# First weights of the heads' values loaded and split inside the last seven-product units

## The chip, the cores and the metric

The kernel runs on one core of one Trainium2 chip. The metric is the device time of one execution in microseconds (us); the median over several runs counts. Five engines work side by side, each on its own queue, in order: TensorE (PE: matmuls and transposes, with its weight loads on PEld), VectorE (DVE), ScalarE (ACT), GpSimd (POOL) and SyncE (SP), which here only issues loads.

## The reference

One layer of a streaming-encoder trunk, 1024 tokens of width 1024, all in float32. What matters here is the start of it:

```python
h = rms_norm(x, g_mix[l])
proj = h @ w_in[l]
c_h, c_b, c_c, sq, sk, sv, xq, gate_pre = jnp.split(proj, split_idx, axis=-1)
...
kv = mem_n @ w_mem_kv
```

`sv` are the values of the 16 heads of the stick-breaking attention, 1024 tokens by 1024 columns. `mem_n` are 256 normalised memory tokens, and `kv` their keys and values for a second attention. After the mixers come a merge, an output product and an MLP.

## The kernel before

**Three matmuls a product.** Each float32 operand is split in a high half (a cast to fp32r) and a low half (the operand less the high half); a product is then three matmuls: high by high, high by low, low by high. For a weight piece of 128 x 1024, `load` (L83) issues the DMA on SP into a buffer `raw` (four exist), and `split_w` makes the high half on ACT (L89) and the low half on DVE (L90). `unit(src, True)` is a load with its split into two pages. A page is a buffer of 128 x 1024, `pg` in the profile; 40 exist. A buffer that is taken again waits until its last reader is done.

**The units.** Most columns of `proj` come from a class `Unit`: a 2 x 2 block product by seven products instead of eight (`p1` to `p7`, L284 to L288), each of 12 matmuls 128x512. The blocks of h are called 11, 21, 12, 22 (second digit: which half of the tokens), and T1 to T4 are sums and differences of them. T1 and T2 are read only by the pair `p6`, `p5`. A unit's own halves of the weights are made by `w1` to `w4`; all of these, and the copies and additions behind each product, go through helpers that pin their order (`order`, L240 on DVE, L243 on ACT).

**The drive.** `Drive.run` walks through a list of (pair, unit). The last six entries of the first drive, of 13 units, are (1,11), (1,12), (2,11), (2,12), (3,11), (3,12): the pairs `p1 p2`, `p6 p5` and `p7 p3`, and `p4` behind pair 3. So the products at the end are p6, p5 of unit 11, p6, p5 of unit 12, then p7, p3, p4 of unit 11 and p7, p3, p4 of unit 12. After the first and second product of each entry, `hook(n, 0)` and `hook(n, 1)` are called. A hook calls `late(n - NP, i)`, if there is one, and then a step of `fin`, the work that a unit leaves to DVE and ACT (here two products of whole pages, two scalings, four shifted additions L596, two more products, and stores). The first drive has no `late`; the second, in the MLP, has one.

```python
                hook(n, 0)
                ...
                second()
                hook(n, 1)
                if k == 3:
                    un.p4()
                    ends.append(un.fin())
```

**Behind the drive.** The block 12 comes back from DRAM (`h12scr`, two loads) and is split by ACT and DVE. Then `v_steps` makes the values: for each of two column groups, four weight pieces `w_v[cg, kp]`, and for each of eight token tiles j a product of 24 matmuls (L210 to L212) in a bank `d`, copied out by ACT (`vv`, L778). Token tiles 0 to 3 need the blocks 11 and 21, tiles 4 to 7 the blocks 12 and 22. The memory tokens (`in_mem`, two loads on SP) are squared on ACT (L157), normalised by DVE, POOL and DVE (L146, L150, L159), and then transposed on TensorE (L176) in between the tiles' matmuls. Loads and splits of `w_kv` follow, and of the second group of `w_v`.

The splits of `w_v` behind the drive are not pinned (`pin[0] = False`); there a scheduler chooses each engine's order.

Of the kernel before, what the change touches and what calls it, by code (L numbers as in the profile page):

```python
# [42 lines left out]
def block_kernel(ctx, tc, x, mem, small, w_in, w_v, w_kv, w_co, w_so, w_xo, w_out, w_up, w_dn, out):  # L43
# [15 lines left out]
    def nm(s):  # L59
        uid[0] += 1  # L60
        return f"{s}_{uid[0]}"
# [7 lines left out]
    def pd():  # L69
        return ps_d.tile([P, 512], F32, tag="d", name=nm("d"))  # L70
# [10 lines left out]
    def load(src):  # L81
        raw = rawp.tile([P, 1024], F32, tag="raw", name=nm("raw"))
        nc.sync.dma_start(out=raw, in_=src)  # L83
        return raw
# [11 lines left out]
    def halves(raw, paged=False):  # L96

        if paged:
            hl = (page(), page())
        else:  # L100
            w = whlp.tile([P, 2, 1024], F32R, tag="whl", name=nm("whl"))
            hl = (w[:, 0, :], w[:, 1, :])
        split_w(raw, hl)
        return hl

    def unit(src, paged=False):

        return halves(load(src), paged)
# [20 lines left out]
    def cut(hl, a, b):  # L129
        return (hl[0][:, a:b], hl[1][:, a:b])  # L130
# [22 lines left out]
    def normed(src):  # L153

        ss = stat(1)
        xn = page(F32)
        nc.scalar.activation(xn, src, AF.Square, accum_out=ss)  # L157
        r = rstd(ss, 1, D)
        nc.vector.tensor_scalar_mul(xn, src, r)  # L159
        return xn  # L160
# [45 lines left out]
    def mm3_steps(ps, pairs, cuts=2):  # L206

        n = len(pairs)
        for i, ((ah, al), (bh, bl)) in enumerate(pairs):
            nc.tensor.matmul(ps, lhsT=ah, rhs=bh, start=i == 0, stop=False)  # L210
            nc.tensor.matmul(ps, lhsT=ah, rhs=bl, start=False, stop=False)  # L211
            nc.tensor.matmul(ps, lhsT=al, rhs=bh, start=False, stop=i == n - 1)  # L212
            if (i + 1) % (n // cuts) == 0:
                yield
# [283 lines left out]
    sec_h = Seconds(C_GMIX, h12_scr)  # L498

    def hx(k, th):  # L500

        return sec_h.h[("11", "12", "21", "22")[2 * (k // 4) + th]][k % 4]
# [114 lines left out]
    def a_(sec, rows, kk):  # L617
        return lambda: sec.second_a(rows, kk)

    def b_(sec, kk):  # L620
        return lambda: sec.second_b(kk)

    def weaving(sec, rows):

        hooks = {at: a_(sec, rows, kk) for kk, at in enumerate(((0, 1), (1, 0), (1, 1), (2, 0)))}
        hooks.update({(4 + kk // 2, kk % 2): b_(sec, kk) for kk in range(4)})
        return hooks

    xrows = load_rows(x, 0, 4)
    dr = Drive(units)  # L630
# [2 lines left out]
    xrows = load_rows(x, 512, 4)  # L633
    run(sec_h.first(rows0))
    rows1 = [normed(t) for t in xrows]
    dr.run(weaving(sec_h, rows1))
    pin[0] = False


# [117 lines left out]

    def v_steps():

        us = [unit(w_v[0, kp], True) for kp in range(4)]  # L760
        for cg in range(2):
            un = []
            for j in range(8):
                if cg == 0 and j >= 4:
                    un.append(unit(w_v[1, j - 4], True))
                ps = pd()
                yield from mm3_steps(
                    ps,
                    [
                        (  # L770
                            cut(hx(k, j // 4), (j % 4) * P, (j % 4) * P + P),
                            cut(us[k // 2], (k % 2) * 512, (k % 2) * 512 + 512),
                        )
                        for k in range(KT)
                    ],
                )
                vv = hpp.tile([P, 512], F32, tag="hp", name=nm("vv"))
                nc.scalar.copy(vv, ps)  # L778
                nc.gpsimd.dma_start(
                    out=v_scr[cg][:, :, j * P : (j + 1) * P], in_=vv.rearrange("p (a e) -> p a e", a=4)  # L780
                )
            us = un
# [163 lines left out]

    nxt = {}
    vgen = v_steps()
    fill(vgen, 2)
    mts = [normed(t) for t in load_rows(mem, 0, NM)]  # L950
# [190 lines left out]
    for ch in range(2):  # L1141
# [3 lines left out]
        for t in range(8):  # L1145
            th, i = t // 4, t % 4
# [183 lines left out]
```

## Time and profile before

| | us |
|---|---|
| median of 3 runs | 2228.43 |
| lowest and highest | 2228.33, 2230.82 |
| the profiled execution | 2230.86 |
| its span, first to last instruction | 2229.2 |

The profiled execution has its own time, 1.7 us longer than its span, and 2.4 us above the median of the three runs. In the rows of a timeline the first number is the start in us from the span's start, the second the duration (of all of a merged group, where a count such as x2 stands at the end), and in brackets the idle time of the engine ahead of it with what ended that. In a table by windows the numbers behind the stretch are its length, the busy time of PE, PEld, DVE, ACT and, where it did anything, POOL, each with a count of instructions, then the granted clock of TensorE as a share of full speed, the DMA engines' mean busy share, and GB/s.

### The profile page before, as it was taken

Reading aid. Unit: us, or ns where it says so; the run is one execution under the profiler, and the core shown is the slowest. Engines: PE = TensorE matmul, PEld = TensorE weight load, DVE = VectorE, ACT = ScalarE, POOL = GpSimd, SP = SyncE. Lnnn points to the kernel's source line nnn. Section 1 sums busy time; section 2 is a strip of 40 time slices with the busy share of each in tenths; the row PEclk is TensorE's granted clock in tenths of the full one; section 3 lists DMA queues with packets and bytes.
Section 4 is the critical chain, followed back from the end, with each engine's and each line's share of the span. In section 5 each row is a group of like instructions: output and inputs, shape, how many; then the busy total and the mean of one; then the engine's idle time right before and its main releaser. Section 6 shows DMA issues by size and latency. Waiting matters only on the chain.

```text
span 2229.2 us, 27032 instructions
## 1 busy us (share of the span) xinstructions
PE 2164.5 (97%) x10148; PEld 1789.0 (80%) x10148; DVE 1405.1 (63%) x1891; ACT 1002.9 (45%) x1789; POOL 383.8 (17%) x574
## 2 busy tenths in 40 slices
PE   7999989999999999999999999999989999999999
PEld 5788869888888788778888788888868888788887
DVE  6555552265778778778777534442576565777776
ACT  6333243354656555555655321121555555433332
POOL 1000011122333333333333000000112211200000
PEclk9999999999999999999999999999999999999999
DMA  4322243232312222321221445334234444744444
GB/s 170 132 66 76 84 173 126 82 122 90 99 67 65 90 74 60 94 75 57 91 80 68 150 151 161 104 95 161 104 133 165 147 148 171 265 162 142 142 151 142
DMA packets 75011, 263.94 MB, mean 118 GB/s; under 512 B 9856, under 2 KB 9856, under 8 KB 74880
## 3 DMA queue, kind: packets, MB, share of 16 engines
q1 hardware_dynamic: 53824, 190.37, 26.6%
q0 software_dynamic: 21056, 71.84, 8.5%
q8 instruction: 80, 1.31, 0.2%
q14 instruction: 51, 0.42, 0.1%
HBM read 181.95 MB, written 71.83 MB: 114 GB/s over the span
## 4 chain that ended last, share of the span: by engine, by line
PE 72%; DVE 11%; issue 7%; ACT 6%; POOL 4%; DMA 1%; POOLq 0%; ACTq 0%; DVEq 0%; SPq 0%
PE d L211 6%; PE d L212 6%; PE d L210 6%; PE d L287 6%; PE d L288 6%; PE d L284 6%; PE d L126 4%; PE d L127 4%; PE d L125 4%; PE z L288 4%; PE z L284 4%; PE z L287 4%; DVE pg L240 3%; POOL pg L847 2%; DVE pg L114 2%
## 5 line engine op out<-in xcount | busy, mean ns | idle before, releaser
L210 PE MATMUL d<-pg,whl 128*128 128x512 f32 x736 | 294.6, 400 | 0.1
L243 ACT ACTIVATE pg<-pg 128x512 f32<-128x512 f32 (+1 forms) x192 | 150.6, 790 | 306.2 <-DVE pg L240 293.5
L211 PE MATMUL d<-pg,whl 128*128 128x512 f32 x736 | 288.1, 391 | 0.0
L212 PE MATMUL d<-pg,whl 128*128 128x512 f32 x736 | 288.1, 391 | 0.0
L847 POOL TENSOR_SCALAR_AFFINE_SELECT pg<-pg 128x128 f32<-128x128 f32 x256 | 168.8, 666 | 282.1 <-ACT pg L844 270.8
L857 DVE TENSOR_TENSOR_SCAN pg<-pg,zero 128x128 f32<-128x128 f32 (+7 forms) x128 | 177.1, 1383 | 57.2 <-POOL pg L847 54.5
L240 DVE TENSOR_TENSOR pg<-pg,pg 128x1024 fp32r<-128x1024 f32 (+3 forms) x180 | 183.5, 1030 | 46.6 <-ACT pg L243 42.9
L113 ACT CAST pg<-t 128x256 fp32r<-128x256 f32 (+2 forms) x336 | 115.1, 368 | 203.3 <-DVE pg L114 144.7
L284 PE MATMUL d<-pg,whl 128*128 128x512 f32 x420 | 166.3, 396 | 7.3 <-ACT pg L243 7.3
L287 PE MATMUL d<-pg,whl 128*128 128x512 f32 x420 | 166.4, 396 | 4.4 <-DVE pg L240 3.4
L288 PE MATMUL d<-pg,whl 128*128 128x512 f32 x420 | 165.4, 394 | 0.8 <-DVE whl L240 0.8
L212 PEld LDWEIGHTS d<-pg,whl 128*128 128x128 f32 x736 | 138.3, 188 | 30.7
L210 PEld LDWEIGHTS d<-pg,whl 128*128 128x128 f32 x736 | 138.4, 188 | 25.2 <-ACT ox L755 0.5
L211 PEld LDWEIGHTS d<-pg,whl 128*128 128x128 f32 x736 | 138.5, 188 | 24.3
L284 PE MATMUL z<-pg,whl 128*128 128x512 f32 x396 | 156.0, 394 | 0.0
L287 PE MATMUL z<-pg,whl 128*128 128x512 f32 x396 | 155.5, 393 | 0.0
L288 PE MATMUL z<-pg,whl 128*128 128x512 f32 x396 | 155.4, 392 | 0.0
L90 DVE TENSOR_TENSOR whl<-raw,whl 128x1024 fp32r<-128x1024 f32 x78 | 99.1, 1271 | 83.1 <-ACT whl L89 82.4
L89 ACT CAST whl<-raw 128x1024 fp32r<-128x1024 f32 x78 | 82.5, 1058 | 152.8 <-DMA raw<-in_w_co 47.9
L127 PE MATMUL d<-pg,whl 128*128 128x512 f32 x384 | 149.5, 389 | 0.5 <-DVE whl L90 0.5
L125 PE MATMUL d<-pg,whl 128*128 128x512 f32 x384 | 149.5, 389 | 0.1
L126 PE MATMUL d<-pg,whl 128*128 128x512 f32 x384 | 149.4, 389 | 0.0
(200 smaller groups left out, 4799.7 us busy)
## 6 DMA issues: line engine op xcount, KB each, us to landing
raw<-in_w_in SPq DMA_DIRECT2D x76, 512.0 KB, 3.6
raw<-in_w_up SPq DMA_DIRECT2D x36, 512.0 KB, 3.6
pg<-in_w_dn SPq DMA_DIRECT2D x32, 512.0 KB, 4.8
raw<-fscr_s SPq DMA_DIRECT2D x32, 512.0 KB, 3.6
gscr<-pg POOLq DMA_DIRECT2D x24, 512.0 KB, 2.9
raw<-gscr SPq DMA_DIRECT2D x24, 512.0 KB, 4.0
fscr<-pg POOLq DMA_DIRECT2D x48, 256.0 KB, 2.8
fscr_s<-pg POOLq DMA_DIRECT2D x48, 256.0 KB, 3.3
```

What stands on the lines that cost most here:

```text
L125: nc.tensor.matmul(ps, lhsT=ah, rhs=bh, start=i == 0, stop=False)
L126: nc.tensor.matmul(ps, lhsT=ah, rhs=bl, start=False, stop=False)
L127: nc.tensor.matmul(ps, lhsT=al, rhs=bh, start=False, stop=i == n - 1)
L210: nc.tensor.matmul(ps, lhsT=ah, rhs=bh, start=i == 0, stop=False)
L211: nc.tensor.matmul(ps, lhsT=ah, rhs=bl, start=False, stop=False)
L212: nc.tensor.matmul(ps, lhsT=al, rhs=bh, start=False, stop=i == n - 1)
L240: order(nc.vector.tensor_tensor(out=out, in0=a, in1=b, op=op))
L284: m_ = nc.tensor.matmul(ps, lhsT=ah, rhs=bh, start=first and i == 0, stop=False, **go)
L287: nc.tensor.matmul(ps, lhsT=ah, rhs=bl, start=False, stop=False, **go)
L288: nc.tensor.matmul(ps, lhsT=al, rhs=bh, start=False, stop=i == n - 1, **go)
L847: nc.gpsimd.affine_select(out=t_[:, W - P : W], in_=t_[:, W - P : W], pattern=[[-1, P]], compare_op=ALU.is_gt, fill=fill_, base=0, channel ...
L857: nc.vector.tensor_tensor_scan(out=rev, data0=rev, data1=zero.broadcast_to([P, W]), initial=1.0, op0=ALU.mult, op1=ALU.add)
```

## The change

The first drive gets a `late` function. In the last two entries of the list, (3,11) and (3,12), it calls `unit` on one piece of the first group of `w_v` behind each of p7 and p3: piece 0 behind p7 of unit 11, piece 1 behind p3 of unit 11, piece 2 behind p7 of unit 12, piece 3 behind p3 of unit 12. `v_steps` takes these four instead of loading its own. At that point T1 and T2 have been read for the last time, so pages are free. `pin[0]` is still true there, so the four casts and the four subtractions keep their places among the units' work.

```diff
     rows1 = [normed(t) for t in xrows]
-    dr.run(weaving(sec_h, rows1))
+    us0 = []
+
+    def v_ahead(n, i):
+
+        if n >= -2:
+            us0.append(unit(w_v[0, 2 * (n + 2) + i], True))
+
+    dr.run(weaving(sec_h, rows1), v_ahead)
     pin[0] = False
...
-        us = [unit(w_v[0, kp], True) for kp in range(4)]
+        us = us0
```

On DVE at the end of the first drive the difference reads as follows. L90 with `raw` is the subtraction that makes a low half of a weight piece (raw_1919, 1939, 1972, 1993 are pieces 0 to 3); `d_1760` is the bank of unit 11 behind p7, `z_1851` its bank behind p3, `d_1796` and `z_1888` the same of unit 12; the row that writes pg_1917 is the low half of unit 12's block A22, for p4 of unit 12; the two rows of 128x1024 pages without `raw` are the first step of `fin` of unit 11.

```order
 L240 TENSOR_TENSOR pg_1915<-d_1760,pg_1844 128x512
+L90 TENSOR_TENSOR pg_1922<-raw_1919,pg_1921 128x1024
 L240 TENSOR_TENSOR pg_1917<-raw_1700,pg_1917 128x512
 L240 TENSOR_TENSOR pg_1794<-z_1851,pg_1844 128x512
-L240 TENSOR_TENSOR pg_1958<-d_1796,pg_1878 128x512
+L90 TENSOR_TENSOR pg_1942<-raw_1939,pg_1941 128x1024
+L240 TENSOR_TENSOR pg_1970<-d_1796,pg_1878 128x512
+L90 TENSOR_TENSOR pg_1975<-raw_1972,pg_1974 128x1024
 L240 TENSOR_TENSOR pg_1794<-pg_1794,pg_1675 128x1024
 L240 TENSOR_TENSOR pg_1915<-pg_1915,pg_1729 128x1024
 L240 TENSOR_TENSOR pg_1830<-z_1888,pg_1878 128x512
+L90 TENSOR_TENSOR pg_1996<-raw_1993,pg_1995 128x1024
```

The four subtractions stood behind all of this, behind `fin` of both units and behind the four subtractions of block 12; now each stands behind the addition of one product. After the last row shown come three of the shifted additions, the subtraction of the first piece of `w_kv`, the fourth shifted addition, two products of pages and the four subtractions of block 12. On ACT the casts of pieces 0 and 1 now follow the high half of A22 of unit 12, those of 2 and 3 the copy of p4 of unit 11.

On SP, in the same place, the loads now stand so (raw_2022 and 2024 are block 12, raw_2129 and 2131 the first pieces of `w_kv`, raw_2249 is the first piece of the second group of `w_v`):

```order
+L83 DMA raw_1919<-in_w_v 128x1024
+L83 DMA raw_1939<-in_w_v 128x1024
+L83 DMA raw_1972<-in_w_v 128x1024
+L83 DMA raw_1993<-in_w_v 128x1024
+L83 DMA raw_2022<-h12scr_116 128x1024
+L83 DMA raw_2024<-h12scr_117 128x1024
 L83 DMA raw_2129<-in_w_kv 128x1024
 L83 DMA raw_2131<-in_w_kv 128x1024
+L83 DMA raw_2249<-in_w_v 128x1024
 L166 DMA pg_2109<-in_mem 128x1024
 L166 DMA pg_2111<-in_mem 128x1024
-L83 DMA raw_2249<-in_w_v 128x1024
```

Block 12 was loaded first and the four pieces behind it; now the pieces go first, and one piece of the second group stands ahead of the memory tokens' loads. That piece goes into the buffer that the first piece of `w_kv` leaves.

On TensorE, before, the first matmul of each of the token tiles 0, 1 and 2 stood at the head, then the other 23 of tile 0; now tile 0 runs with its 24 matmuls in a row, then tile 1, and the first two transposes of the memory tokens stand one matmul ahead of the end of tile 2, two more five matmuls of tile 3 later. From the second half of tile 3 on, every engine has the same instructions in the same order as before.

## The prediction

> **What bounds the kernel now.** I read the page first, then TensorE's waits from the end of the first drive (286 us) to 520 us, a table of windows around its two longest, and last the order of time of each engine there. The page's busy table:
>
> ```profile
> PE 2164.5 (97%) x10148; PEld 1789.0 (80%) x10148; DVE 1405.1 (63%) x1891; ACT 1002.9 (45%) x1789; POOL 383.8 (17%) x574
> ```
>
> TensorE is the bound; DVE and ACT have room. A change is worth what it takes from TensorE's gaps. The five longest waits between 286 and 520 us (sum, times, longest one):
>
> ```profile
> PE d L211 <- DVE pg L90: 4.4, 1, 4.4
> PE d L210 <- ACT pg L89: 3.7, 1, 3.7
> PE t L699 <- POOL pg L691: 1.2, 1, 1.2
> PE t L699 <- DVE pg L114: 0.5, 1, 0.5
> PE d L126 <- DVE pg L114: 0.4, 1, 0.4
> ```
>
> The first two are for the subtraction (L90) and the cast (L89) of weight piece 0 of the values. The windows around them:
>
> ```profile
> 288.05:291.91 3.86, 0.17 (x2) 0.01 (x1) 3.82 (x4) 3.66 (x7) 0.00 (x0) 1.00 0.00 0
> 291.91:297.26 5.35, 0.96 (x3) 0.48 (x3) 5.35 (x8) 0.90 (x1) 1.06 (x2) 0.59 0.60 196
> 297.26:302.98 5.72, 5.72 (x14) 4.42 (x14) 2.95 (x3) 2.52 (x3) 0.00 (x0) 0.50 1.00 386
> ```
>
> While TensorE stands, DVE works nearly throughout (3.82 of 3.86 us, 5.35 of 5.35). Behind the waits the granted clock is 0.50 for 5.72 us, and there the DMA engines are full (share 1.00). TensorE's own rows, the first of them the last matmul of the drive, the others token tile 0 with two strays:
>
> ```profile
> 287.82 0.39 PE L288 MATMUL d<-pg,pg 128*128 128x512 f32 x1
> 291.91 0.96 PE L210 MATMUL d<-pg,pg 128*128 128x512 f32 x3 [3.69 <-ACT pg L89]
> 297.26 0.80 PE L211 MATMUL d<-pg,pg 128*128 128x512 f32 x1 [4.40 <-DVE pg L90]
> 297.86 0.63 PE L212 MATMUL d<-pg,pg 128*128 128x512 f32 x1
> ...
> 302.98 0.48 PE L212 MATMUL d<-pg,pg 128*128 128x512 f32 x1
> 303.30 0.39 PE L210 MATMUL d<-pg,pg 128*128 128x512 f32 x1
> ...
> 305.14 0.39 PE L212 MATMUL d<-pg,pg 128*128 128x512 f32 x1
> ```
>
> The row at 291.91 holds the first matmul of tiles 0, 1 and 2; the one at 305.14 is the 24th and last of tile 0. Between these two ends lies the whole loss. Why the halves come so late stands on DVE:
>
> ```profile
> 274.65 0.69 DVE L240 TENSOR_TENSOR pg<-d,pg 128x512 f32<-128x512 f32 x1 [2.04 <-PE d L288]
> 275.26 0.68 DVE L240 TENSOR_TENSOR pg<-raw,pg 128x512 fp32r<-128x512 f32 x1
> 277.37 0.69 DVE L240 TENSOR_TENSOR pg<-z,pg 128x512 f32<-128x512 f32 x1 [1.43 <-PE z L288]
> 282.81 0.69 DVE L240 TENSOR_TENSOR pg<-d,pg 128x512 f32<-128x512 f32 x1 [4.75 <-PE d L288]
> 283.42 2.35 DVE L240 TENSOR_TENSOR pg<-pg,pg 128x1024 f32<-128x1024 f32 x2
> 285.69 0.68 DVE L240 TENSOR_TENSOR pg<-z,pg 128x512 f32<-128x512 f32 x1
> 286.29 5.11 DVE L596 SCALAR_TENSOR_TENSOR pg<-pg,sm,pg 128x1023 f32<-128x1023 f32 x4
> ...
> 293.58 2.49 DVE L240 TENSOR_TENSOR pg<-raw,pg 128x512 fp32r<-128x512 f32 x4
> 295.99 2.35 DVE L90 TENSOR_TENSOR pg<-raw,pg 128x1024 fp32r<-128x1024 f32 x2
> ...
> 308.13 0.76 DVE L159 TENSOR_SCALAR pg<-pg,st 128x1024 f32<-128x1024 f32 x1 [0.75 <-POOL st L150]
> ```
>
> From 283.42 on DVE does `fin` of units 11 and 12, then block 12 (293.58), then pieces 0 and 1 (295.99). Ahead of that it idles 4.75 us. ACT and SP in the same stretch:
>
> ```profile
> 272.43 0.62 ACT L243 ACTIVATE pg<-raw 128x512 fp32r<-128x512 f32 x1
> 280.09 0.60 ACT L243 ACTIVATE pg<-d 128x512 f32<-128x512 f32 x1 [7.04 <-PE d L288]
> 284.67 2.29 ACT L243 ACTIVATE pg<-pg,sm 128x1024 f32<-128x1024 f32 x2 [3.98 <-DVE pg L240]
> 288.25 0.60 ACT L243 ACTIVATE pg<-d 128x512 f32<-128x512 f32 x1 [1.29 <-PE d L288]
> 288.74 2.18 ACT L243 ACTIVATE pg<-raw 128x512 fp32r<-128x512 f32 x4
> 290.82 1.99 ACT L89 CAST pg<-raw 128x1024 fp32r<-128x1024 f32 x2
> 299.81 1.05 ACT L89 CAST pg<-raw 128x1024 fp32r<-128x1024 f32 x1 [7.00 <-DMA raw<-in_w_v]
> ...
> 306.05 1.06 ACT L157 ACTIVATE pg<-pg 128x1024 f32<-128x1024 f32 x1
> ```
>
> ```profile
> 262.97 5.21 SPq L83 DMA_DIRECT2D raw<-h12scr  x2
> 272.64 23.79 SPq L83 DMA_DIRECT2D raw<-in_w_v  x4
> 297.24 1.47 SPq L83 DMA_DIRECT2D raw<-in_w_kv  x2
> 298.75 0.93 SPq L166 DMA_DIRECT2D pg<-in_mem  x2
> ```
>
> And the times from issue to landing (shortest, median, longest), of `in_w_v` and of `in_mem`:
>
> ```profile
> DMA to landing us min/median/max: 3.4/4.7/5.5
> ...
> DMA to landing us min/median/max: 6.3/6.7/7.1
> ```
>
> **The change: what the gap costs now.** A product of twelve matmuls takes 277.37 − 274.65 = 2.72 us, so one takes 0.227 us. Without a gap the matmul after 287.82 starts at 288.05. Up to 305.14 there are 25 matmuls (three first ones and 22 more of tile 0), 25 x 0.227 = 5.67 us: the last of tile 0 would start at 293.72. The loss is 305.14 − 293.72 = 11.4 us. In parts: first wait 291.91 − 288.05 = 3.86; second 297.26 − 291.91 less three matmuls, 4.67; half clock, 14 matmuls in 303.30 − 297.26 = 6.04 instead of 3.18, 2.86; the remaining eight lose 0.02.
>
> The clock part has a page beside it. The Trainium skill, "TensorE: Matmul & The Clock Gate", Part 1, says that the array falls to half rate after an idle window of about 3.4 us and comes back after about as much sustained work. The trace agrees in kind (waits of 3.86 and 4.67 us, then 0.50), but the half rate lasts 6.04 us of work; by the page's 3.4 us that term would be 1.7 us instead of 2.86, and the sum 10.3.
>
> **Are the pieces there in time?** Piece by piece, with the durations above (1.05 a cast, 1.23 a subtraction, 0.68 half of one, 1.28 a shifted addition, 1.18 a product of pages).
>
> Loads. SP now issues piece 0 where block 12's first load went, at 262.97, and piece 1 at the second, 5 us later. Piece 2 goes at 272.64. Piece 3 takes the buffer that piece 0 leaves. With 5.5 us to land, pieces 0 and 1 are there by 273.4, and piece 2 by 278.2.
>
> Pieces 0 and 1. ACT idles 7.04 us ahead of 280.09; the casts run behind the row at 272.43, from 273.05 (piece 1 from 274.1) to 275.2. On DVE the subtraction of piece 0 follows the row at 274.65, to 276.6. That pushes the half of A22 from 275.26 to 276.6; p4 of unit 12 needs it at 288.05 − 2.72 = 285.3, so this costs nothing. Piece 1 follows the row at 277.37, to 279.3. No product waits for either.
>
> Pieces 2 and 3. Piece 3 is issued at 276.6 and lands by 282.1. The casts stand behind the row at 280.09, which keeps its time: 280.7 to 281.8, and to 283.2. DVE takes piece 2 behind the row at 282.81, to 284.8; then two products (287.1), the addition of p3 (287.8), piece 3 to 289.0. TensorE needs piece 3 from the 19th matmul of tile 0, 288.05 + 18 x 0.227 = 292.1. Margin 3.1 us. All four casts and subtractions are in the old idle time or behind work that TensorE no longer waits for. If the cover were gone, every microsecond of piece 3 past 292.1 would be one lost.
>
> What is late next: the memory tokens' first transpose. TensorE reaches it after 71 matmuls, at 288.05 + 71 x 0.227 = 304.2. Its loads stand on SP behind both `w_kv` pieces and, new, a piece of the second group that takes the buffer of the first `w_kv` piece. That one is loaded when piece 2 has left its buffer (284.8), lands by 290.3, is cast behind the drive's last copy (288.25) and half of block 12, and is subtracted behind three shifted additions: 289.0 + 3.84 + 1.23 = 294.1. Then the piece and the memory tokens go, the latter from 294.5, 4.2 us before today's 298.75. Landing between 3.4 and 7.1 us later, 297.9 to 301.6, and ACT is free at 299.8 behind the copy of tile 1 (ends at 288.05 + 48 x 0.227 = 298.9). From squaring to the normalised row takes 308.13 + 0.76 − 306.05 = 2.84 us: 302.6 to 304.4. The wait is between 0 and 0.2 us; I take 0, since the DMA engines that made today's 7.1 full are less full when the four pieces have gone ahead.
>
> Block 12 is loaded behind piece 3 and split by DVE behind `fin`, at 294.1 + 1.28 + 2.35 + 2.49 = 300.2; token tile 4 needs it at 288.05 + 96 x 0.227 = 309.8 at the earliest. POOL's stores of unit 12 hold nothing up that TensorE reads.
>
> From tile 3 on the order on every engine is as before, so all later work is 11.4 us earlier. What the trace can't show is whether later waits change. They were 1.2, 0.5 and 0.4 in the first list, so at best another 2.1 us goes; at worst the transposes' wait above or the one of rival A. I take 0, as nothing there has another order.
>
> Sum: 11.4 us off the profiled execution, 2230.86 − 11.4 = 2219.5. That execution lies 2.4 above the median of the runs, with the same work; off the median 2228.43 it is **2217.0 us**, 0.5% less.
>
> **Rivals.** *A, part of it is given back at the memory tokens.* If their loads go no earlier than today, 298.75, with the median landing 6.7 and 2.84 behind it, the first row is ready at 308.3, and TensorE stands 4.1 us at the transposes: gain 7.3, 2221.1. If the clock falls as it did behind waits of 3.86 and 4.67, another 2.86 goes: 2224.0. For it: they queue on SP behind one load more. Against: that load's buffer is free at 294.1. By the section of the Trainium skill named above a wait of 4.1 us is long enough to cost the half rate, for 3.4 us, which gives 2222.8.
>
> *B, nothing comes of it.* The stage behind is held by its loads (share 1.00 in the third window), and all 11.4 us return as waits for `w_kv`: 2228.4. Against it: after the two waits the list has no DMA and nothing over 1.2 us.
>
> *C, slower.* The subtraction of piece 0 now stands ahead of A22's half on DVE, and the drive's last product waits for that. If piece 0's load is late, the drive itself stops at 285.3. Free up to a landing at 285.3 − 0.68 − 1.23 − 1.05 = 282.3; slower than before from 282.3 + 11.4 − 2.86 (the half clock again) = 290.9 on, 27.9 us after issue. At 33 us it would be 2233.5. The longest landing shown is 7.1 us, so only a buffer that comes free much later than 262.97 could do it.
>
> **The numbers.** Forecast 0.80, A 0.12, B 0.05, C 0.03. The forecast's own range goes from 2217.0 − 2.1 = 2214.9 to 2217.0 + 2.4 = 2219.4, the upper end if the runs lie as far above their lowest as the profiled execution did; from there I reach into A as far as 2222.0, which leaves out the half clock of A, B and C. 0.2% is 4.5 us, about what a measurement of this kernel can tell from no change. Faster: the forecast and nearly all of A, 0.91; same: B and the worst of A, 0.06; slower: C, 0.03.
>
> **What would show it.** Right: the last matmul of p4 of unit 12 and the first of tile 0 stand 0.23 us apart; the waits for L89 and L90 are gone from the list; the granted clock is 1.00 from 288 to 306; the last matmul of tile 0 starts near 293.3. The memory tokens' loads are issued at about 294.5, and no wait over 0.5 us stands at the first L176. Wrong: a new wait of TensorE at L176 (A), waits for `w_kv` between 310 and 500 (B), a wait at p4 of unit 12 (C), or a piece 3 that comes after 292.

## The result and the profile after

| | before | after |
|---|---|---|
| median of 6 runs each, us | 2229.97 (2228.33 to 2230.82) | 2216.28 (2214.35 to 2217.17) |
| the profiled execution, us | 2230.86 | 2216.34 |
| its span, us | 2229.2 | 2214.4 |

The ratio is 0.9941, with a 95% interval of 0.9930 to 0.9951. The forecast was 2217.0, in a range of 2214.9 to 2222.0. The sum behind it was 11.4 us; the medians differ by 13.7. Where the other 2.3 come from is a question of its own, below.

TensorE's waits of the kernel after, in a window that begins inside the drive and ends behind the values (sum, times, longest):

```profile
PE t L706 <- POOL pg L698: 1.2, 1, 1.2
PE t L706 <- DVE pg L114: 0.4, 1, 0.4
PE d L126 <- DVE pg L114: 0.4, 1, 0.4
```

The two longest waits of before, for L89 and L90, are gone. These three are the small ones of before, with other line numbers. Windows of the kernel after over the old gap, up to the memory tokens, and one that runs on:

```profile
288.05:293.30 5.25, 5.25 (x25) 4.35 (x24) 5.21 (x5) 2.38 (x5) 0.00 (x0) 1.00 0.33 100
293.30:306.00 12.70, 12.70 (x59) 10.46 (x59) 7.30 (x12) 5.34 (x11) 4.38 (x7) 1.00 0.90 329
300.00:330.00 30.00, 30.00 (x150) 24.75 (x149) 12.41 (x18) 13.18 (x23) 4.11 (x7) 1.00 0.64 219
```

TensorE is busy for every microsecond of them, at a granted clock of 1.00. TensorE's rows at the end of the drive, at the end of tile 0 and at the memory tokens' transposes:

```profile
287.23 0.39 PE L288 MATMUL d<-pg,pg 128*128 128x512 f32 x1
287.45 0.39 PE L210 MATMUL d<-pg,pg 128*128 128x512 f32 x1
...
292.67 0.39 PE L212 MATMUL d<-pg,pg 128*128 128x512 f32 x1
...
303.55 0.38 PE L176 MATMUL t<-ident,pg 128*128 128x128 f32 x2
```

The first matmul of tile 0 starts 0.22 us behind the last of p4, the 24th (292.67) after another 23 x 0.227. The transposes have no bracket, so no wait. DVE in the same stretch:

```profile
274.05 0.69 DVE L240 TENSOR_TENSOR pg<-d,pg 128x512 f32<-128x512 f32 x1 [2.04 <-PE d L288]
274.66 1.22 DVE L90 TENSOR_TENSOR pg<-raw,pg 128x1024 fp32r<-128x1024 f32 x1
275.80 0.68 DVE L240 TENSOR_TENSOR pg<-raw,pg 128x512 fp32r<-128x512 f32 x1
276.77 0.69 DVE L240 TENSOR_TENSOR pg<-z,pg 128x512 f32<-128x512 f32 x1 [0.30 <-PE z L288]
277.38 1.22 DVE L90 TENSOR_TENSOR pg<-raw,pg 128x1024 fp32r<-128x1024 f32 x1
282.21 0.69 DVE L240 TENSOR_TENSOR pg<-d,pg 128x512 f32<-128x512 f32 x1 [3.62 <-PE d L288]
282.82 1.22 DVE L90 TENSOR_TENSOR pg<-raw,pg 128x1024 fp32r<-128x1024 f32 x1
...
286.83 1.21 DVE L90 TENSOR_TENSOR pg<-raw,pg 128x1024 fp32r<-128x1024 f32 x1
...
301.10 0.76 DVE L159 TENSOR_SCALAR pg<-pg,st 128x1024 f32<-128x1024 f32 x1 [0.75 <-POOL st L150]
```

Each of the four subtractions follows the addition of a product without standing, so no piece was late for DVE; the idle time ahead of the rows at 276.77 and 282.21 has shrunk from 1.43 and 4.75 to 0.30 and 3.62. SP:

```profile
262.37 13.86 SPq L83 DMA_DIRECT2D raw<-in_w_v  x4
276.50 2.45 SPq L83 DMA_DIRECT2D raw<-h12scr  x2
284.06 4.33 SPq L83 DMA_DIRECT2D raw<-in_w_kv  x2
292.91 0.33 SPq L83 DMA_DIRECT2D raw<-in_w_v  x1
293.29 0.90 SPq L166 DMA_DIRECT2D pg<-in_mem  x2
```

The memory tokens' loads go at 293.29, 5.5 us before the 298.75 of before (4.9 us earlier counted from the drive's end).

**A measure for one region.** The device time holds the scatter of the whole kernel, so the experiments are also read by a difference inside one trace: from the last matmul of the drive (L288) to the store of token tile 3 (the fourth `vscr` row on POOL) or, where the tiles' order differs, to the last of the 16 such stores. The fourth, of before and of after:

```profile
323.37 0.71 POOL L779 DMA_DIRECT2D vscr<-vv  x1 [5.28 <-ACT vv L778]
```

```profile
311.39 0.71 POOL L786 DMA_DIRECT2D vscr<-vv  x1 [5.57 <-ACT vv L785]
```

They are 11.98 apart, of which 287.82 − 287.23 = 0.59 was there at the drive's end. The region itself is 11.39 us shorter.

### The profile page after: what moved, and what is told of

Read it like the earlier page. It is cut to its first block, busy times and chain, and to the rows that moved or that the text cites. A ratio compares the mean times of both kernels' runs of the same rounds, so it can differ in the third digit from the quotient of the medians.

```text
span 2214.4 us, 27027 instructions
## 1 busy us (share of the span) xinstructions
PE 2158.8 (97%) x10148; PEld 1785.1 (81%) x10148; DVE 1404.9 (63%) x1891; ACT 1002.5 (45%) x1789; POOL 383.7 (17%) x574
## 4 chain that ended last, share of the span: by engine, by line
PE 71%; DVE 10%; issue 7%; ACT 6%; POOL 4%; DMA 1%; POOLq 0%; ACTq 0%; SPq 0%; DVEq 0%
PE d L210 6%; PE d L212 6%; PE d L211 6%; PE d L287 6%; PE d L288 6%; PE d L284 6%; PE d L126 4%; PE d L127 4%; PE d L125 4%; PE z L288 4%; PE z L284 4%; PE z L287 4%; POOL pg L854 3%; DVE pg L240 2%; DVE pg L114 2%
## 5 line engine op out<-in xcount | busy, mean ns | idle before, releaser
L288 PE MATMUL d<-pg,whl 128*128 128x512 f32 x420 | 165.1, 393 | 1.0 <-DVE whl L240 1.0
L288 PE MATMUL z<-pg,whl 128*128 128x512 f32 x396 | 154.7, 391 | 0.0
L89 ACT CAST whl<-raw 128x1024 fp32r<-128x1024 f32 x78 | 82.5, 1058 | 152.3 <-DMA raw<-in_w_co 55.1
L90 DVE TENSOR_TENSOR whl<-raw,whl 128x1024 fp32r<-128x1024 f32 x78 | 99.1, 1270 | 78.6 <-ACT whl L89 78.1
```

## The experiments

The theory: DVE does the drive's leftovers (`fin` and block 12) ahead of the pieces' subtractions, and TensorE waits for those; splitting the pieces inside the last products takes the whole gap of 11.4 us away. Its rivals: the loads, not the splits, were late; a quarter of the gap (2.86 us) was the half clock, a term that can be won by itself; part of the gain is given back at the memory tokens; a piece that is late inside the drive costs more than it brings.

Eight experiments ran, in two batches, each batch on one chip with the kernel before beside it. Medians in us; the region's gain is against the first profile of before. The ratio and its interval come from all the runs, and are not the quotient of the two medians (for c2 that would be 0.9959).

| kernel | median (lowest to highest) | before beside it | ratio, 95% interval | region, us |
|---|---|---|---|---|
| c0, before again | 2230.04 (2225.42 to 2231.37) | 2230.08 | 1.0000, 0.9991 to 1.0008 | 0.05 |
| c1, the change again | 2218.72 (2214.32 to 2221.18) | 2230.08 | 0.9948, 0.9934 to 0.9961 | 11.41 |
| e1, two pieces only | 2223.06 (2220.95 to 2223.42) | 2230.08 | 0.9969, 0.9957 to 0.9980 | 9.02 |
| e2, splits behind the drive | 2229.08 (2225.68 to 2230.35) | 2230.08 | 0.9995, 0.9986 to 1.0003 | 1.92 |
| c2, the change a third time | 2221.67 (2216.10 to 2222.39) | 2230.89 | 0.9951, 0.9939 to 0.9964 | 11.41 |
| e5, splits ahead of the leftovers | 2222.28 (2219.53 to 2223.53) | 2230.89 | 0.9962, 0.9949 to 0.9974 | 8.72 |
| e4, one entry earlier | 2219.30 (2217.02 to 2220.46) | 2230.89 | 0.9947, 0.9935 to 0.9960 | 10.37 |
| e3, matmuls in the gap | 2230.13 (2228.22 to 2232.70) | 2230.89 | 0.9998, 0.9989 to 1.0007 | 0.38 |

The starts behind the last column (the drive's last L288, then the fourth store; the sixteenth where that is said): before 287.82, 323.37, sixteenth 437.03; c0 287.98, 323.48; c1 288.13, 312.27; c2 287.30, 311.44; e1 287.77, 314.30; e2 287.70, 321.33; e5 287.69, sixteenth 428.18; e4 287.90, 313.08; e3 288.92, 324.09. The gain of e1, say, is 323.37 − 314.30 less 287.82 − 287.77.

**c0, c1, c2: both kernels again.** No edit.

> The kernel before, unchanged, to see how far its stages move between executions. Theory (the change is worth 11.4 us at the end of the first drive, and what the first comparison shows beyond that is scatter): no difference from before beyond 0.1%, and its rows behind the first drive move by 0.2 to 1 us against the earlier profile at places that no edit touched. Rival (the scatter is below 0.3 us everywhere, so the rest belongs to the change): all rows behind 300 us keep their distances to 0.3 us.

> The changed kernel, unchanged, timed against before in five rounds. Theory: 11.4 us faster by the region at the end of the drive, measured 11 to 13 us; in its profile the last transpose of the memory tokens' first half stands 11.4 us earlier than in before, counted from the drive's end, and distances behind that move by up to 1 us against the first profile of the change. Rival (the change also takes 2 to 3 us from later stages): 13.5 us or more, with the same later steps as in the first profile.

> The changed kernel a third time, for the next three kernels to be read against on the same chip. Theory (11.4 us at the end of the drive, and the rest scatter of later stages): 11.4 us faster in the rows up to the fourth token tile, counted from the drive's end, and 10 to 13.5 us in the measured median. Rival (the first comparison's 13.7 us belongs to the change): 13.5 us again.

The region's gain repeats to 0.02 us in three profiles of the change (11.39, 11.41, 11.41) and is 0.05 for the unchanged kernel. The gain of the medians does not: 13.7, 11.4 and 9.2 us, the last below the 10 to 13.5 that were expected (by the ratios 13.2, 11.6 and 10.9). The five times of c2 are 2216.10, 2216.34, 2221.67, 2222.04 and 2222.39, so its median hangs on one run. The change is worth 11.4 where it was made, and what the medians show above or below comes from other stages.

That the rest is not the change's own shows behind the values. From the sixteenth `vscr` store to the end of the span it takes 1789.3, 1793.4 and 1789.1 us in the three profiles of the change, 1792.2 in before and in c0, and 1789.8 in e3, whose program behind the values is that of before. Short and long ends come with and without the change. The profile of c0 alone would have spoken for its rival: its stores between 300 and 1900 us stand 0.1 to 0.5 us later than those of before, where the drive already ended 0.16 later.

One stage that scatters can be pointed at, 140 us behind the change. There TensorE runs 16 small matmuls (`ones`, 128x1) between two groups of the work behind the values. From the last `vscr` store to the first `oscr` store it takes 451.01 − 425.06 = 25.95 us in the first profile after, 453.95 − 425.93 = 28.02 in c1 and 450.26 − 425.10 = 25.16 in c2, of one program (before: 26.20). A window that begins 1.3 to 1.4 us behind the first of these matmuls, of the first profile after, of c1 and of c2:

```profile
433.00:443.00 10.00, 10.00 (x58) 9.24 (x58) 5.07 (x16) 3.25 (x9) 1.66 (x1) 0.83 0.33 107
```

```profile
434.00:444.00 10.00, 10.00 (x50) 9.29 (x51) 3.75 (x11) 2.59 (x8) 1.66 (x1) 0.69 0.27 95
```

```profile
433.00:443.00 10.00, 10.00 (x69) 8.98 (x70) 5.10 (x16) 3.94 (x12) 1.66 (x1) 1.00 0.31 107
```

TensorE is busy throughout in all three, but the granted clock is 0.83, 0.69 and 1.00, and 58, 50 and 69 matmuls start. Up to 2.9 us of scatter come from this one place. The other differences between the first pair of profiles (0.59 us before the drive's end, some 1.0 between 1093 and 1552 us, some 0.6 near 1650) were only located, not explained.

**e1: two pieces only.** Pieces 0 and 1 go ahead, 2 and 3 stay behind.

```diff
-        if n >= -2:
+        if n == -2:
...
-        us = us0
+        us = us0 + [unit(w_v[0, kp], True) for kp in (2, 3)]
```

> Only pieces 0 and 1 are loaded and split inside the last units, pieces 2 and 3 behind block 12 as before. TensorE then has the first 12 matmuls of tiles 0, 1 and 2 to do, about 35 x 0.227 = 8 us, until piece 2's low half comes at about 297.2 (block 12's four halves to 296.0 on DVE, then 1.23). Theory (what counts is that DVE's first subtraction no longer stands behind the units' leftovers, and that TensorE has work until the rest comes): 10 to 11 us faster than before, a wait under 1 us at 296 to 298, the clock stays at 1.00. Rival (all four pieces are needed in time, since tile 0 goes first): TensorE stops at the 13th matmul, 290.8, until 297.2, the clock halves, and the gain is 2 to 5 us.

```profile
295.93 0.61 PE L210 MATMUL d<-pg,pg 128*128 128x512 f32 x2
...
297.21 0.50 PE L211 MATMUL d<-pg,pg 128*128 128x512 f32 x1 [0.21 <-DVE pg L90]
...
305.55 0.41 PE L176 MATMUL t<-ident,pg 128*128 128x128 f32 x2 [1.70 <-DVE st L146]
```

These are TensorE's only waits of e1 between 287 and 308 us. Piece 2 came at 297.2 and cost 0.21: the order that the scheduler chose does the first twelve matmuls of tile 0, then those of tiles 1 and 2, which need only pieces 0 and 1. So two pieces cover twelve matmuls on each of three tiles. The 1.70 at L176 is the mechanism of the prediction's rival A, at its place. Why the memory tokens are late stands on SP and on ACT of e1:

```profile
294.85 1.53 SPq L83 DMA_DIRECT2D raw<-in_w_kv  x2
296.43 1.24 SPq L166 DMA_DIRECT2D pg<-in_mem  x2
```

```profile
302.57 1.06 ACT L157 ACTIVATE pg<-pg 128x1024 f32<-128x1024 f32 x1 [1.10 <-DMA pg<-in_mem]
```

Their loads go at 296.43 instead of 293.29, because both `w_kv` pieces ahead of them stand until DVE has split block 12, at 293.53 + 2.49 = 296.02:

```profile
293.53 2.49 DVE L240 TENSOR_TENSOR pg<-raw,pg 128x512 fp32r<-128x512 f32 x4
```

In the change the `w_kv` pieces went out as the subtractions of pieces 2 and 3 ended, at 284.04 and 288.04. ACT stands 1.10 us for the DMA. A gain of 9.0 lies between the two figures on record. The rival (a late piece 2 brings back a wait and the half clock) fails, since the clock stays at 1.00; the theory's figure left out the memory tokens.

A wait costs TensorE a little more than its bracket says: a row lasts 0.39 us, but the next matmul starts 0.227 behind it, so another 0.16 is lost ahead of the idle time. With that e1 loses 0.37 + 1.86 of 11.4, which leaves 9.2 (measured 9.0).

**e2: loads early, splits late.** The four pieces are asked for behind the drive and its `fin`, ahead of block 12, with pinned order. The loads still go out early, since their buffers are free.

Against the kernel before:

```diff
     dr.run(weaving(sec_h, rows1))
+    us0 = [unit(w_v[0, kp], True) for kp in range(4)]
...
-        us = [unit(w_v[0, kp], True) for kp in range(4)]
+        us = us0
```

> All four pieces are loaded as early as in the change, but their splits stand right behind the whole drive, behind the leftovers of units 11 and 12 and ahead of block 12, in a fixed order. Theory (the place of the subtractions on DVE decides, not the loads): first low half at about 294.8 instead of 297.2, so 2.4 to 3 us faster than before, the two waits still there with about 1.8 and 4.3 us, and the half clock behind them. Rival (the early loads are what the change gains by): about 11 us faster, as the change itself.

SP, DVE, TensorE and two windows of e2:

```profile
262.85 13.33 SPq L83 DMA_DIRECT2D raw<-in_w_v  x4
```

```profile
286.17 5.11 DVE L596 SCALAR_TENSOR_TENSOR pg<-pg,sm,pg 128x1023 f32<-128x1023 f32 x4
291.19 2.35 DVE L240 TENSOR_TENSOR pg<-pg,pg 128x1024 f32<-128x1024 f32 x2
293.46 4.62 DVE L90 TENSOR_TENSOR pg<-raw,pg 128x1024 fp32r<-128x1024 f32 x4
```

```profile
289.71 0.96 PE L210 MATMUL d<-pg,pg 128*128 128x512 f32 x3 [1.62 <-ACT pg L89]
294.74 0.79 PE L211 MATMUL d<-pg,pg 128*128 128x512 f32 x1 [4.06 <-DVE pg L90]
...
308.20 0.30 PE L176 MATMUL t<-ident,pg 128*128 128x128 f32 x1 [0.65 <-DVE st L146]
```

```profile
289.71:294.74 5.03, 0.96 (x4) 0.49 (x4) 4.99 (x6) 2.79 (x3) 1.06 (x2) 0.77 0.19 77
294.74:299.17 4.43, 4.43 (x11) 3.46 (x11) 3.35 (x3) 0.00 (x0) 0.00 (x0) 0.50 0.97 324
```

The loads were as early as in the change (262.85 against 262.37), and the region gains 1.9 us instead of 11.4. What was late is the place of the subtraction in DVE's row: piece 0 stands behind four shifted additions and two products of `fin`, until 293.46. The wait of 4.06 us is followed by 11 matmuls at 0.50. The gain is below the 2.4 to 3 us that were expected: from the starts the three waits cost 1.78, 4.35 and 0.81, the half clock 1.93, which leaves 2.5 of 11.4; 0.6 us have no place. In the medians' ratio (0.9986 to 1.0003) it can't be told from no change.

**e5: splits ahead of the leftovers.** The pieces are asked for behind the last p4, but ahead of what is left of `fin`, and of block 12. Nothing is done inside the last entries.

```diff
+            if late:
+                late(0, 0)
             for e in ends:
                 run(e)
...
-        if n >= -2:
-            us0.append(unit(w_v[0, 2 * (n + 2) + i], True))
+        if n == 0:
+            us0.extend(unit(w_v[0, kp], True) for kp in range(4))
```

> All four pieces are split behind the drive's last product, but ahead of what units 11 and 12 have left for DVE (the four shifted additions and two products of pages) and ahead of block 12. Casts from 288.75 on, first low half at about 291.0, the others 1.15 apart. Theory (a few microseconds of other work ahead on DVE are what TensorE waits for; waits below 2 us leave the clock at 1.00): two waits of about 1.6 and 0.5 us, no half clock, 9 us faster than before at the fourth token tile. Rival (what counts is that the splits lie inside the drive, under its products): 2 to 3 us faster, as with the splits right behind the leftovers.

```profile
289.68 4.63 DVE L90 TENSOR_TENSOR pg<-raw,pg 128x1024 fp32r<-128x1024 f32 x4 [3.44 <-ACT pg L89]
```

```profile
289.70 0.96 PE L210 MATMUL d<-pg,pg 128*128 128x512 f32 x3 [1.62 <-ACT pg L89]
290.96 0.50 PE L211 MATMUL d<-pg,pg 128*128 128x512 f32 x1 [0.30 <-DVE pg L90]
```

```profile
288.00:292.00 4.00, 2.08 (x9) 1.36 (x9) 2.32 (x3) 3.88 (x5) 0.00 (x0) 1.00 0.06 9
```

Against e2 only the leftovers changed sides, and the second wait falls from 4.06 to 0.30 us, with no half clock behind it: the region gains 8.7. So DVE's leftovers were what TensorE waited for. The first wait is unchanged at 1.62; it is for the cast, which stands on ACT behind the drive's last copy, as it does in e2. That part goes only when the pieces stand inside the drive. From the starts, the two waits cost 1.78 and 0.58, which leaves 9.0 of 11.4; 0.3 us have no place.

**e4: one entry of the list earlier.** All four pieces move from entries (3,11), (3,12) to (2,12), (3,11).

```diff
-        if n >= -2:
-            us0.append(unit(w_v[0, 2 * (n + 2) + i], True))
+        if -3 <= n < -1:
+            us0.append(unit(w_v[0, 2 * (n + 3) + i], True))
```

> The four pieces are split one entry of the list earlier: piece 0 behind p6 of unit 12, piece 1 behind p5, pieces 2 and 3 behind p7 and p3 of unit 11. Piece 2 then goes into the buffer that piece 0 leaves at about 273 and lands at 277 to 279, and DVE stands at its subtraction ahead of the half of A22 and of the addition of p3. Theory (TensorE needs that half only at 285.3, so DVE may stand for 6 us): the same time as the change to 0.1%, no wait of TensorE inside the drive. Rival (the drive's own work must not stand behind a load): a wait of TensorE at p4 of unit 12 or at a bank, 1 to 4 us slower than the change.

ACT, DVE and TensorE of e4:

```profile
277.07 1.05 ACT L89 CAST pg<-raw 128x1024 fp32r<-128x1024 f32 x1 [2.82 <-DMA raw<-in_w_v]
```

```profile
278.15 1.22 DVE L90 TENSOR_TENSOR pg<-raw,pg 128x1024 fp32r<-128x1024 f32 x1 [2.27 <-ACT pg L89]
...
300.87 0.15 DVE L146 TENSOR_SCALAR st<-st 128x1 f32<-128x1 f32 x1 [3.71 <-ACT pg L157]
```

```profile
302.67 0.41 PE L176 MATMUL t<-ident,pg 128*128 128x128 f32 x2 [0.56 <-DVE st L146]
```

This is the mechanism of rival C in small: a piece isn't there when its cast is due, and ACT stands 2.82 us and DVE 2.27 inside the drive. TensorE has no wait there, so a stand of 2.3 us is still covered; how long one would hurt was not tried. The region gains 10.4, 1.0 less than the change, of which 0.56 + 0.16 are the new wait at the memory tokens. That wait isn't rival A: their loads go at 289.18, earlier than in the change. But TensorE's order has the first transposes after 61 matmuls instead of 71, and ACT squares the tokens (L157) only from 299.69, behind the copy of tile 1. By the ratios of the times the two kernels can't be told apart (0.9947 against 0.9951).

**e3: matmuls in the gap.** The kernel before, with 40 more matmuls 128x512 behind block 12's split in the program. Nobody reads what they write.

```diff
     settle()
+    idle = pt()
+    for _ in range(40):
+        order(nc.tensor.matmul(idle, lhsT=sec_h.h["11"][0][0][:, 0:P], rhs=sec_h.h["11"][0][0], start=True, stop=True))
```

> The kernel before, with 40 matmuls more that nobody reads, put behind the drive so that TensorE works through the gap (40 x 0.227 = 9.1 us, to about 297.1). The clock then stays at 1.00, the weights come as before. Theory (the half clock hid the late pieces 2 and 3, whose low halves come at 302.1 and 303.6): tile 0 stops for piece 2, and the gain is 0.3 to 1 us. Rival (the half clock is a term of its own, 2.9 us of the 11.4): 2.5 to 3 us faster than before.

```profile
289.15 9.23 PE L650 MATMUL t<-pg 128*128 128x512 f32 x40
...
302.05 0.73 PE L210 MATMUL d<-pg,pg 128*128 128x512 f32 x2 [0.92 <-ACT pg L89]
303.31 0.50 PE L211 MATMUL d<-pg,pg 128*128 128x512 f32 x1 [0.29 <-DVE pg L90]
```

```profile
297.20:303.00 5.80, 4.88 (x21) 3.30 (x19) 3.21 (x3) 1.68 (x2) 0.00 (x0) 1.00 0.99 341
```

The clock stays at 1.00, and yet the region gains only 0.4 us of the 2.86 that the half clock had cost. TensorE now reaches the later pieces sooner than they are ready, and stands 0.92 and 0.29 us for them, with ACT standing 7.03 us for the load of `w_v`, up to 300.95. From the starts these two waits take 1.07 and 0.46 us. Another 0.53 go to the edit itself: the first matmuls of tiles 0, 1 and 2, which before ran inside the gap, now stand behind the 40. That leaves 0.8 of 2.86, where 0.4 was measured. So the half clock of before hid the lateness of the later pieces: the terms of the loss add up, but not each of them can be won alone.

## Why the prediction was right

**The sum.** A loss of 11.4 us between 288.05 and 305.14 was to go whole. The region became 11.39 to 11.41 us shorter in three profiles, so this step held to 0.02 us. Taken from the starts of rows, not from the brackets, it had the extra 0.16 of every wait in it.

**The cause.** DVE's leftovers ahead of the subtractions, and not the loads alone, made the pieces late. e2 and e5 show it: with equally early loads the gain is 1.9 behind the leftovers and 8.7 ahead of them. The loads matter too, for pieces 2 and 3: in e3, with the loads of before, TensorE stands 0.92 and 0.29 us for these. No run splits early with loads as late as before.

**The cover.** The four casts and subtractions were to lie in old idle time. They do: piece 3 was ready at 286.83 + 1.21 = 288.04, and needed at 287.45 + 18 x 0.227 = 291.5. The margin is 3.5 us (predicted 3.1). The half of A22 that piece 0 pushed back, to 275.80, cost nothing; e4 shows that even 2.3 us of standing inside the drive cost TensorE nothing there.

**The clock.** The granted clock was to be 1.00 from 288 to 306, and it was. Across the kernels, the waits of 1.62 and 1.70 us kept 1.00, and a stretch at 0.50 came with the waits of before and of e2. Windows of 0.1 us show where it began: in before at 292.9, behind the three matmuls that follow the wait of 3.69, and in e2 at 292.4, 1.7 us into the wait of 4.06. In the stage of the `ones` matmuls no wait was longer than 1.2. So these runs give no length below which a wait is safe. The Trainium skill, "TensorE: Matmul & The Clock Gate", Part 1, puts the idle window at about 3.4 us; the waits of 1.62 and 1.70 agree, while the fall 1.7 us into a wait shows that the length of one wait doesn't decide. For the way back that page of the Trainium skill gives at least one busy window of about 3.4 us; here it was 4.43 us of work in e2 and 5.72 in before, so the single 3.4 of the prediction's comparison is too short. It would have made the predicted sum 10.3; the region's 11.4 decides for the rows.

**Rival A.** The memory tokens were to go at about 294.5, and the first normalised row to be ready at 302.6 to 304.4. They went at 293.29, the row was ready at 301.10 + 0.76 = 301.86, and the transposes at 303.55 didn't wait. The mechanism is real all the same: the waits at L176 in e1 (1.70) and e2 (0.65), whose loads go at 296.43 and 298.50, are it, and the change escapes by 1.7 us. Rival B is refuted by the list of TensorE's waits, in which none is for `w_kv`, and by the window from 300 to 330 us, busy throughout; rival C by the drive's end, which has no wait.

**The size.** The sum was taken off the lowest-lying median, that of three runs at 2228.43. The median of six is 2229.97, from which 11.4 would give 2218.6, while 2216.28 was measured. A base 1.5 too low and a scatter of 2.3 in the change's favour cancelled to within 0.7 of the forecast of 2217.0, and that is luck. The three medians of the change (2216.28, 2218.72, 2221.67) lie on both sides of the forecast, so its last 2 us were not to be had: they are scatter of other stages. The range holds all three.

## What to carry to other kernels

When TensorE waits for a split, look first at what stands ahead of it on the splitting engine's row: early loads brought little (1.9 us here, with the splits also ahead of block 12) while the splits were queued behind leftovers that TensorE didn't wait for. Add up the loss from the starts of matmuls, with the slow stretch behind the waits in it, but don't count on winning its terms one by one. And when a change moves loads, follow the load behind them on the same queue; here the memory tokens', gone out late, gave part of the lead back in two of the variants.

## What the runs showed of the hardware

One program's TensorE clock behind the same small wait came out in three ways. In all three profiles of the change the stage with the 16 matmuls of `ones` has a longest wait of 1.2 us, and then a clock of 0.83, 0.69 or 1.00 over 10 us. A stage of 25.2 us takes up to 2.9 us longer without any change in its work.

The half rate came in steps. In windows of 0.1 us the stretches at 0.50 lasted 10.2 to 10.3 us at the gap of before and c0, 6.9 at that of e2, and in the stage of `ones` 3.4 or 3.5 us (before, c0, after, e4), 6.8 or 6.9 (c1, e1, e2, e5) or nothing (c2, e3): about one, two or three times 3.4 us. That stage took 25.2 us without a stretch, 25.95 to 26.28 with the short one, and 27.4 to 28.0 with the long one, so its scatter goes by the number of steps. The Trainium skill, "TensorE: Matmul & The Clock Gate", Part 1, says that the window of about 3.4 us runs freely, and that its phase shifts from run to run; the steps have that length, but no run here shows the window itself.
